# Last expert pair and output rows of a hybrid block: two quarters of the down product in a row, last rows scaled by VectorE

## The chip, the cores and the metric

The kernel is one launch on one core of a Trainium2 chip. The metric is the device time of a run in microseconds (us). PE is TensorE (matrix products into PSUM), DVE is VectorE, ACT is ScalarE, POOL is GpSimd, and SP is the engine that here only issues DMAs. Each engine takes its instructions in the order in which they were written, and waits on semaphores where an operand comes from another engine or from a DMA.

## The reference, cut to what matters

The input is 256 tokens of width 1024. Attention and a state-space mixer come first and are not touched. The end is a mixture of experts, then a gated projection and a norm:

```python
x = x + (gate_a * y_a + gate_b * y_b) @ w_out[i]
h2 = rms_norm(x, ffn_norm_g[i])
x = x + hier_moe(h2, ...)          # 16 experts: out += combine[e] * (silu(h @ w_gate[e]) * (h @ w_up[e])) @ w_down[e]
x = x + jax.nn.sigmoid(x @ w_ple_gate[i]) * (p[i] @ w_ple_proj[i])
return rms_norm(x, final_norm_g)
```

## The kernel before, in words

Tokens lie in two tiles of 128 (index `i`). The 16 experts are worked through in 8 pairs. For each pair the kernel gathers up to 64 tokens an expert, multiplies by gate and up (`gate_up`, L1078), transposes the hidden activations (`hidden_T`, L1097 and L1098), multiplies by down, splits the result into a rounded high part `yh` and a remainder `yl`, and scatters both back into four PSUM banks `x2_0` to `x2_3` (tile 0 and 1, left and right half of the columns) with a one-hot matrix. A pair's scatter (L1125) stands in the next pair's turn.

The last pair is done by quarters of 256 columns. `q_down(q)` is the down product of a quarter (L1429) with ACT making `yh` (L1434) and DVE making `yl` (L1435). `q_x2(q)` scatters it (L1441) and lets DVE add the residual `xt` (L1445). `q_T(q)` transposes the new residual (L1451) and splits it into `x2h` on ACT (L1453) and `x2l` on DVE (L1454). Then the gate product `x @ w_ple_gate` can use that quarter as rows of its contraction: its weights come in eight blocks `pg_0` to `pg_7` (block c has quarter c % 4 of the rows, and half c // 4 of the columns). `pg_split(c)` rounds a block on ACT (`wh_pg`, L329) and takes the remainder on DVE or, for blocks 4, 1 and 6, on POOL (`wl_pg`, L332). `pg(c, i, j)` issues the three products high by high, high by low, low by high (L341 to L343) for two rows of blocks.

`pg_gate` is the sigmoid (ACT, L1479), the product with `p @ w_ple_proj` and the sum with `xt` (DVE, L1480 and L1481). `pg_sq` squares and sums (ACT, L1490, for the last quarter DVE, L1488), `pg_sum` adds the parts (L1493), `pg_pow` raises to the power -1/2 on POOL (L1498), `pg_gain` multiplies by the norm's gain (L1501), and `finish` scales by the row's factor and stores: left half on ACT (L1505), right half on DVE (L1506), stores (L1509) by SP, and for the left half of tile 1 by ACT. The right half of tile 1 is done in two quarters (j = 0 and 1), the second one in a bank of its own, `pge`.

Behind all this stands a branch (L1155) that skips the work for experts with more than 64 tokens. PE, ACT, DVE and POOL each carry it, and SP then waits for all stores and all engines (L1599).

The order is the order of the calls in the code. Weights are streamed by SP alone, in the order of a list (`pending`), in which `LAST` says which gate blocks follow each quarter of down. A DMA is issued when a buffer of the ring of 51 is free and the eighth DMA before it has landed.

Of the kernel before, what the change touches and what calls it, by code (L numbers as in the profile page):

```python
# [11 lines left out]
AF = mybir.ActivationFunctionType  # L12
# [13 lines left out]
NPAIR = NE // 2  # L26
WARM = 10
PG_POOL = (4, 1, 6)
LAST = ((4,), (0,), (5, 1), (2, 6, 3, 7))
DFF = 512  # L30
IF_ENGINES = [mybir.EngineType.PE, mybir.EngineType.Activation, mybir.EngineType.DVE, mybir.EngineType.Pool]
IN_DIM = 6160
# [58 lines left out]
def emit(ctx, tc, ring, x, p, mix_norm_g, w_in, conv_w, conv_b, dt_bias,  # L91
# [1023 lines left out]
            dve.scalar_tensor_tensor(mo["yl"][:, sl], by[hf], cw, mo["yh"][:, sl].bitcast(F32), op0=OP.mult,  # L1115
                                     op1=OP.subtract)

    def scatter(pr, mo, st, tiles):
        for i in tiles:
            for hf in range(2):  # L1120
                for n, y in enumerate(("yh", "yl")):
                    j, first = 2 * i + hf, pr == 0 and n == 0
                    if first:
                        bx[j] = bank(j, f"x2_{j}")
                    pe.matmul(bx[j], st[:, i * P:(i + 1) * P], mo[y][:, 512 * hf:512 * hf + 512],  # L1125
                              start=first, stop=False, skip_group_check=True)
# [258 lines left out]
    for pr in range(NPAIR):  # L1385
        if pr == 2:
            MO["most"] = nc.values_load(cnt[0:1, 16:17], IF_ENGINES, min_val=0, max_val=T)
        if 0 < pr < NPAIR - 2 and pr % 2 == 0:
            for i in range(2):
                onehots(pr // 2 + 1, i)  # L1390
        st, cw = gate_up(pr, mo, first_pair() if pr == 0 else None)
        if pr % 2 == 1:
            XT[pr // 2].free()
        for i in range(2):

            if pr == 1:
# [12 lines left out]
        if pr == 0:  # L1409
            pp_end()  # L1410
        if pr < NPAIR - 1:
            down(pr, mo, cw)
        pend = (pr, st)
    table(AF.Sigmoid)
    MO["S"].free()
# [7 lines left out]
        return slice(256 * q, 256 * q + 256)  # L1423

    def q_down(q):
        b = bank(4, f"y7{q}")
        for c in range(4):
            for s in range(2):
                pe.matmul(b[64 * s:64 * s + 64, 0:256], mo["hT"][:, c, 64 * s:64 * s + 64],  # L1429
                          ready[f"d{NE - 2 + s}_{q}"][0][:, c, :], start=(c == 0), stop=(c == 3), skip_group_check=True)  # L1430
        for s in range(2):
            consumed(f"d{NE - 2 + s}_{q}")
        h, l = mo["yh"][:, quarter(q)], mo["yl"][:, quarter(q)]
        act.activation(h, b[:, 0:256], AF.Copy, scale=cw)  # L1434
        dve.scalar_tensor_tensor(l, b[:, 0:256], cw, h.bitcast(F32), op0=OP.mult, op1=OP.subtract)  # L1435
# [37 lines left out]
    def pg_cols(hf, j):  # L1473
        return slice(512 * hf, 512 * hf + 512) if j is None else quarter(2 * hf + j)

    def pg_gate(i, hf, j=None):
        sl = pg_cols(hf, j)
        t = sc.t[i][:, sl]
        act.activation(t, pgb[i, hf, j][:, sl.start - 512 * hf:sl.stop - 512 * hf], AF.Sigmoid)  # L1479
        dve.tensor_tensor(t, t, pp["t"][i][:, sl], OP.mult)  # L1480
        dve.tensor_tensor(t, t, xt[i][:, sl], OP.add)  # L1481

    def pg_sq(i, hf, j=None):

        sl, c = pg_cols(hf, j), 32 + 4 * i + hf + (j or 0)
        t, b, a = sc.t[i][:, sl], pgb[i, hf, j][:, sl.start - 512 * hf:sl.stop - 512 * hf], stat[:, c:c + 1]
        if j == 1:
            dve.scalar_tensor_tensor(b, t, 1.0 / D, t, op0=OP.mult, op1=OP.mult, accum_out=a)  # L1488
        else:
# [7 lines left out]
        r = stat[:, 40 + i:41 + i]  # L1497
        pool.tensor_tensor(r, r, nhalf[:, :1], OP.pow)  # L1498

    def pg_gain(i, sl):  # L1500
        dve.tensor_tensor(sc.t[i][:, sl], sc.t[i][:, sl], ready["fng"][0][:, 0, sl], OP.mult)  # L1501

    def finish(i):
        r = stat[:, 40 + i:41 + i]
        act.activation(sc.t[i][:, 0:512], sc.t[i][:, 0:512], AF.Copy, scale=r)  # L1505
        dve.tensor_scalar(sc.t[i][:, 512:1024], sc.t[i][:, 512:1024], r, None, op0=OP.mult)  # L1506
        for h in (1, 0):
            s = slice(512 * h, 512 * h + 512)
            (act if i > h else sp).dma_start(dram(out, i * P * D + 512 * h, [[D, P], [1, 512]]), sc.t[i][:, s])  # L1509

    q_down(0)
    pg_split(4)
    q_x2(0)
    q_T(0)
    pg_split(0)
    q_down(1)
    pg(4, 0)
    pg(4, 1, 0)
    q_x2(1)
    q_T(1)  # L1520
# [52 lines left out]
    for a in [X[0], X[1]] + [MO[n, i] for n in ("h2h", "h2l") for i in range(2)]:
# [29 lines left out]
```

## Time and profile before

| | us |
|---|---|
| median of 3 runs | 502.16 (501.2 to 502.59) |
| profiled execution | 501.87 |
| its span, first to last instruction | 500.1 |
| PE busy in the span | 482.4 |
| DVE, ACT, POOL busy | 208.2, 190.1, 129.7 |

The span is 1.8 us shorter than the profiled execution's time; the rest lies around it. The granted clock of PE was 1.0 from 12 us on until PE had done its last product. The last pair's work begins at about 450 us; everything ahead of it is the same in both kernels. Times below are us from the span's start.

### The profile page before, as it was taken

To read this page: it belongs to the slowest core of one execution; us is meant where nothing else is said; L and a number is where in the kernel's file an instruction comes from. 1 tells how busy PE (TensorE), PEld (TensorE's weight loads), DVE (VectorE), ACT (ScalarE), POOL (GpSimd) and SP (SyncE) were. 2 spreads that over 40 slices of the span, in tenths; PEclk is the share of its full clock that TensorE was granted. 3 is DMA by queue.
4 is the path that set the end of the run, shared out by engine and by line. 5 is a ranking of instruction groups with operands and counts; after the bars stand their busy time and mean duration, and the time that the engine had idled before them with its cause. 6 is when DMAs were issued, how large, how long until landed. Compare 5 with 4: busy or idle time off the path is not lost.

```text
span 500.1 us, 7983 instructions
## 1 busy us (share of the span) xinstructions
PE 482.4 (96%) x3093; PEld 340.5 (68%) x3093; DVE 208.2 (42%) x407; ACT 190.1 (38%) x344; POOL 129.7 (26%) x83
## 2 busy tenths in 40 slices
PE   6999999999999999999999999999999999999992
PEld 6997988999988999988744353434434353335682
DVE  4324678795669484744631111111201010103465
ACT  4747576644686273443531111110202020104442
POOL 3767546333887640060300000000000000001201
PEclk8999999999999999999999999999999999999997
DMA  8899999612323798677658999999999999999602
GB/s 288 233 318 348 348 348 283 209 43 87 102 88 124 256 393 289 207 252 293 251 209 312 368 410 408 409 410 408 409 408 409 408 409 409 409 389 364 222 0 90
DMA packets 71221, 145.25 MB, mean 290 GB/s; under 512 B 8244, under 2 KB 41352, under 8 KB 71176
## 3 DMA queue, kind: packets, MB, share of 16 engines
q1 hardware_dynamic: 70888, 143.89, 79.5%
q10 hardware_dynamic: 288, 0.79, 0.4%
q8 instruction: 26, 0.43, 0.3%
q14 instruction: 19, 0.16, 0.1%
HBM read 143.61 MB, written 1.05 MB: 289 GB/s over the span
## 4 chain that ended last, share of the span: by engine, by line
PE 88%; DVE 6%; ACT 2%; issue 2%; DMA 1%; POOL 0%; DVEq 0%; ACTq 0%; POOLq 0%
PE u L1078 11%; PE g L1078 11%; PE y L1108 10%; PE ac_gb L363 5%; PE ac_ob L363 5%; PE ac_ga L363 5%; PE g L1024 3%; PE ac_xs L363 3%; PE x L1125 3%; PE ac_bc L363 2%; PE ac_q L363 2%; PE ac_z L363 2%; PE ac_k L363 2%; PE y L1429 2%; PE pg L341 1%
## 5 line engine op out<-in xcount | busy, mean ns | idle before, releaser
L332 POOL TENSOR_TENSOR wl_pg<-pg,wh_pg 128x1024 fp32r<-128x1024 f32 x3 | 7.2, 2395 | 226.0 <-PE x L1441 213.7
L1078 PE MATMUL u<-u,XT 128*64 128x512 f32 x256 | 57.2, 595 | 0.0
L1078 PE MATMUL g<-g,XT 128*64 128x512 f32 x256 | 56.8, 593 | 0.0
L1108 PE MATMUL y<-d,mid 128*64 128x512 f32 x224 | 49.6, 595 | 0.0
L1078 PEld LDWEIGHTS g<-g,XT 128*64 128x64 f32 x256 | 18.1, 137 | 35.4 <-issue 32.9
L1078 PEld LDWEIGHTS u<-u,XT 128*64 128x64 f32 x256 | 17.9, 137 | 33.6 <-issue 30.2
L1115 DVE SCALAR_TENSOR_TENSOR yl<-y,cwt,yh 128x512 fp32r<-128x512 f32 x14 | 10.5, 750 | 60.2 <-ACT yh L1114 59.4
L1108 PEld LDWEIGHTS y<-d,mid 128*64 128x64 f32 x224 | 15.5, 137 | 29.4 <-issue 25.7
L1091 DVE SCALAR_TENSOR_TENSOR mid<-u,cwt,mid 128x512 f32<-128x512 f32 x8 | 6.0, 751 | 54.1 <-issue 47.4
L1098 ACT ACTIVATE mid<-hT 128x512 f32<-128x512 f32 x8 | 4.8, 598 | 55.0 <-PE hT L1097 55.0
L1114 ACT ACTIVATE yh<-y,cwt 128x512 fp32r<-128x512 f32 x14 | 9.6, 687 | 40.4 <-PE y L1108 40.4
L332 POOL TENSOR_TENSOR wl_xs<-xs,wh_xs 128x1024 fp32r<-128x1024 f32 x8 | 19.1, 2391 | 17.7 <-ACT wh_xs L329 8.0
L1053 ACT ACTIVATE sT<-st 128x256 fp32r<-128x256 f32 x8 | 3.1, 385 | 54.1 <-DVE cwt L1052 51.7
L1050 DVE COPY cwt<-st 128x1 f32<-128x1 f32 x8 | 1.3, 158 | 42.9 <-PE st L1045 42.9
L711 POOL TENSOR_TENSOR su<-su,su 128x768 f32<-128x768 f32 x8 | 16.9, 2108 | 7.6 <-ACT su L710 7.1
L1024 PE MATMUL g<-S,h2h 128*128 128x256 f32 x60 | 15.4, 291 | 0.6 <-ACT XT L1032 0.6
L332 POOL TENSOR_TENSOR wl_wo<-wo,wh_wo 128x1024 fp32r<-128x1024 f32 x3 | 7.8, 2613 | 31.0 <-ACT wh_wo L329 29.6
L1032 ACT ACTIVATE XT<-g,gfd 128x256 f32<-128x256 f32 x16 | 6.7, 470 | 23.4 <-PE g L1024 22.2
L1024 PE MATMUL g<-S,h2l 128*128 128x256 f32 x60 | 14.8, 281 | 0.0
L1024 PEld LDWEIGHTS g<-S,h2h 128*128 128x128 f32 x60 | 11.3, 188 | 4.1 <-issue 2.4
L332 POOL TENSOR_TENSOR wl_z<-z,wh_z 128x1024 fp32r<-128x1024 f32 x4 | 9.6, 2401 | 16.3 <-ACT wh_z L329 7.1
L341 PE MATMUL pg<-wh_pg,x2h 128*128 128x512 f32 (+1 forms) x32 | 12.3, 383 | 0.0
(392 smaller groups left out, 1178.7 us busy)
## 6 DMA issues: line engine op xcount, KB each, us to landing
g<-in_w_gate_dram SPq DMA_DIRECT2D x64, 512.0 KB, 10.2
u<-in_w_up_dram SPq DMA_DIRECT2D x64, 512.0 KB, 10.2
d<-in_w_down_dram SPq DMA_DIRECT2D x64, 512.0 KB, 10.2
xs<-in_w_in_dram SPq DMA_DIRECT2D x8, 512.0 KB, 8.8
z<-in_w_in_dram SPq DMA_DIRECT2D x8, 512.0 KB, 8.7
ga<-in_w_in_dram SPq DMA_DIRECT2D x8, 512.0 KB, 8.7
gb<-in_w_in_dram SPq DMA_DIRECT2D x8, 512.0 KB, 7.4
ob<-in_w_out_b_dram SPq DMA_DIRECT2D x8, 512.0 KB, 3.4
```

The lines of the kernel that those rows point to most:

```text
L332: (pool if pool_lo else dve).tensor_tensor(l, src, h.bitcast(F32), OP.subtract)
L341: pe.matmul(o, lh, rh, start=start, stop=False, skip_group_check=skip)
L363: pe.matmul(st["b"][:, T * f:T * f + T], w[:, k, 128 * f:128 * f + 128], x_.k(kk), start=(n + kk + f == 0), stop=(n == 2 and kk == 4 * k_u ...
L711: pool.tensor_tensor(e, e, cbm[:, t // 4:t // 4 + 1, :].to_broadcast([P, 2, 384]), OP.mult)
L1024: pe.matmul(b[:, 256 * k:256 * k + 256], MO[hs, i].t[0][:, kk * P:(kk + 1) * P], S, start=(first and n == 0 and k == 0), stop=(last and n ...
L1032: act.activation(o[:, 256 * k:256 * k + 256], b[:, 256 * k:256 * k + 256], AF.Copy, scale=g2[:, k:k + 1])
L1078: pe.matmul(b[64 * s:64 * s + 64, :], xg.k(kk)[:, s0 + 64 * s:s0 + 64 * s + 64], ws[s][:, k, :], start=(kk == 0), stop=(kk == KD - 1), ski ...
L1108: pe.matmul(by[hf][64 * s:64 * s + 64, :], mo["hT"][:, c, 64 * s:64 * s + 64], w[:, 0, 512 * hf:512 * hf + 512], start=(c == 0), stop=(c = ...
L1114: act.activation(mo["yh"][:, sl], by[hf], AF.Copy, scale=cw)
L1115: dve.scalar_tensor_tensor(mo["yl"][:, sl], by[hf], cw, mo["yh"][:, sl].bitcast(F32), op0=OP.mult, op1=OP.subtract)
L1125: pe.matmul(bx[j], st[:, i * P:(i + 1) * P], mo[y][:, 512 * hf:512 * hf + 512], start=first, stop=False, skip_group_check=True)
L1429: pe.matmul(b[64 * s:64 * s + 64, 0:256], mo["hT"][:, c, 64 * s:64 * s + 64], ready[f"d{NE - 2 + s}_{q}"][0][:, c, :], start=(c == 0), sto ...
```

## The change

1. The scatter of pair 6 is issued in another order: left halves of both tiles, the transposes of the hidden activations, the right half of tile 0, and the right half of tile 1 only after the scatter of quarter 0.
2. Quarter 1's down product follows quarter 0's at once, in a bank of its own. `LAST` loads its weights ahead of `pg_4`.
3. Gate products stand between the steps: `pg(4, 0)` ahead of the transposes of quarter 1, `pg(4, 1, 0)` behind them; the scatter of quarter 2 comes ahead of `pg(5, 1, 0)`, not behind.
4. The first quarter of the right half of tile 1 keeps its sum in PSUM (`pg_x3`) and its squares go to SBUF.
5. Tile 0 is scaled by factor and gain in one DVE instruction a half; tile 1 is scaled by DVE alone. ACT's two scales (L1505) are gone. SP issues all four stores.

```diff
-LAST = ((4,), (0,), (5, 1), (2, 6, 3, 7))
+LAST = ((), (4, 0), (5, 1), (2, 6, 3, 7))
...
+        if pr == NPAIR - 1:
+            scatter(pend[0], mo, pend[1], (0, 1), (0,))
+            hidden_T(pr, mo)
+            scatter(pend[0], mo, pend[1], (0,), (1,))
+            break
...
-        b = bank(4, f"y7{q}")
+        b = accbank("y71") if q == 1 else bank(4, f"y7{q}")
...
+    def pg_x3(i, hf, j):
+
+        sl = pg_cols(hf, j)
+        if j != 0:
+            return sc.t[i][:, sl]
+        return pgb[i, hf, j][:, sl.start - 512 * hf:sl.stop - 512 * hf]
+
...
-        dve.tensor_tensor(t, t, xt[i][:, sl], OP.add)
+        dve.tensor_tensor(pg_x3(i, hf, j), t, xt[i][:, sl], OP.add)
...
-    def finish(i):
-        r = stat[:, 40 + i:41 + i]
-        act.activation(sc.t[i][:, 0:512], sc.t[i][:, 0:512], AF.Copy, scale=r)
-        dve.tensor_scalar(sc.t[i][:, 512:1024], sc.t[i][:, 512:1024], r, None, op0=OP.mult)
-        for h in (1, 0):
-            s = slice(512 * h, 512 * h + 512)
-            (act if i > h else sp).dma_start(dram(out, i * P * D + 512 * h, [[D, P], [1, 512]]), sc.t[i][:, s])
+    def store(i, h):
+        s = slice(512 * h, 512 * h + 512)
+        sp.dma_start(dram(out, i * P * D + 512 * h, [[D, P], [1, 512]]), sc.t[i][:, s])
...
     q_down(0)
     pg_split(4)
+    q_down(1)
     q_x2(0)
+    scatter(pend[0], mo, pend[1], (1,), (1,))
     q_T(0)
+    q_x2(1)
     pg_split(0)
-    q_down(1)
     pg(4, 0)
-    pg(4, 1, 0)
-    q_x2(1)
     q_T(1)
     pg_split(5)
+    pg(4, 1, 0)
...
     pg(5, 0)
+    q_x2(2)
     pg(5, 1, 0)
-    q_x2(2)
...
-    finish(0)
+    for h in range(2):
+        s = slice(512 * h, 512 * h + 512)
+        dve.scalar_tensor_tensor(sc.t[0][:, s], sc.t[0][:, s], stat[:, 40:41], ready["fng"][0][:, 0, s], op0=OP.mult,
+                                 op1=OP.mult)
+        store(0, h)
...
+    pg_gain(1, 1, 0)
+    pg_gain(1, 1, 1)
+    for h in (1, 0):
+        s = slice(512 * h, 512 * h + 512)
+        dve.tensor_scalar(sc.t[1][:, s], sc.t[1][:, s], r, None, op0=OP.mult)
+        store(1, h)
```

PE, from the last products of `gate_up` on, in the kernel before (`x_0` to `x_3` are the scatter's banks, `hT` the transposed hidden activations, `y` a quarter of down, `x2T` the transposed residual; each `y` row has seven more like it):

```order
L1125 MATMUL x_1_3233<-yh_3103,sT_3044 128x512
...
L1097 MATMUL hT_4111<-ident,mid_3038 128x128 x4
L1125 MATMUL x_2_3263<-yh_3103,sT_3044 128x512
...
L1125 MATMUL x_3_3266<-yh_3103,sT_3044 128x512
...
L1429 MATMUL y_4122<-d_0_3960,mid_3038 64x256
...
L1441 MATMUL x_0_3230<-yh_3103,sT_3044 128x256
...
L1451 MATMUL x2T_4143<-ident,x_66 128x128 x2
...
L1429 MATMUL y_4156<-d_1_3970,mid_3038 64x256
```

The same place in the changed kernel:

```order
L1097 MATMUL hT_4111<-ident,mid_3038 128x128 x4
L1125 MATMUL x_1_3233<-yh_3103,sT_3044 128x512
...
L1433 MATMUL y_4120<-d_0_3960,mid_3038 64x256
...
L1433 MATMUL y_4135<-d_1_3968,mid_3038 64x256
...
L1445 MATMUL x_0_3230<-yh_3103,sT_3044 128x256
...
L1125 MATMUL x_3_3266<-yh_3103,sT_3044 128x512
...
L1455 MATMUL x2T_4154<-ident,x_66 128x128 x2
```

Both quarters of `y` now stand ahead of the first `x_0` of a quarter, and the products into `x_3` stand between that scatter and the transposes.

ACT at the same place, before:

```order
L1434 ACTIVATE yh_3103<-y_4122,cwt 128x256
L329 ACTIVATE wh_pg_4133<-pg_3968 128x1024
L1453 ACTIVATE x2h_4148<-x2T_4143 128x512
L329 ACTIVATE wh_pg_4152<-pg_3989 128x1024
L1434 ACTIVATE yh_3103<-y_4156,cwt 128x256
```

And in the changed kernel:

```order
L1438 ACTIVATE yh_3103<-y_4120,cwt 128x256
L329 ACTIVATE wh_pg_4131<-pg_3987 128x1024
L1438 ACTIVATE yh_3103<-y_4135,cwt 128x256
L1457 ACTIVATE x2h_4159<-x2T_4154 128x512
L329 ACTIVATE wh_pg_4169<-pg_3989 128x1024
```

The second `yh` now stands ahead of the first `x2h`, behind the rounding of block `pg_4`; on DVE the second `yl` likewise stands ahead of the two residual adds of quarter 0.

DVE at the end, from the last quarter's sum to the branch, before:

```order
L1488 SCALAR_TENSOR_TENSOR pge,stat<-sc_4350 128x256
L1567 TENSOR_TENSOR stat<-stat 128x1
L1501 TENSOR_TENSOR sc_4350<-sc_4350,fng 128x512
L1506 TENSOR_SCALAR sc_4350<-sc_4350,stat 128x512
L1155 COMPARE_AND_BRANCH
```

And in the changed kernel:

```order
L1501 SCALAR_TENSOR_TENSOR pge,stat<-sc_4350 128x256
L1580 TENSOR_TENSOR stat<-stat 128x1
L1515 TENSOR_TENSOR sc_4350<-pg_4191,fng 128x256
L1515 TENSOR_TENSOR sc_4350<-sc_4350,fng 128x256
L1586 TENSOR_SCALAR sc_4350<-sc_4350,stat 128x512 x2
L1155 COMPARE_AND_BRANCH
```

One gain of 512 columns became two of 256, the first of them with its operand in PSUM, and DVE has the left half's scale that ACT had.

## Rows read from the trace of the kernel before

**Rows 1.** Chain of waits: start us, us, engine, tile, line.

```profile
453.28 1.90 PE y L1429 x16
...
455.27 0.48 ACT yh L1434
...
457.98 1.88 PE y L1429 x16
...
460.29 0.23 PE pg L342
...
466.43 1.88 PE y L1429 x16
...
478.86 0.44 PE x2T L1451 x4
```

**Rows 2.** Timeline of PE, transposes of quarter 0; in brackets idle before.

```profile
457.21 0.77 PE L1451 MATMUL x2T<-ident,x 128*128 128x128 f32 x4 [0.28 <-DVE x L1445]
```

**Rows 3.** Groups by line, 443 to 501 us: count, then busy us, mean ns, idle before.

```profile
L329 ACT ACTIVATE wh_pg<-pg 128x1024 fp32r<-128x1024 f32 x8 | 8.3, 1050 | 0.0
...
L332 POOL TENSOR_TENSOR wl_pg<-pg,wh_pg 128x1024 fp32r<-128x1024 f32 x3 | 7.2, 2395 | 226.0 <-PE x L1441 213.7 <-ACT wh_pg L329 12.2
...
L1445 DVE TENSOR_TENSOR x<-x,x 128x256 f32<-128x256 f32 x8 | 3.0, 419 | 4.0 <-PE x L1441 4.0
...
L1454 DVE TENSOR_TENSOR x2l<-x2T,x2h 128x512 fp32r<-128x512 f32 x4 | 2.8, 692 | 3.2 <-ACT x2h L1453 3.1
...
L1453 ACT ACTIVATE x2h<-x2T 128x512 fp32r<-128x512 f32 x4 | 2.4, 598 | 9.5 <-PE x2T L1451 8.1 <-DMA d<-in_w_down_dram 1.3
...
L1435 DVE SCALAR_TENSOR_TENSOR yl<-y,cwt,yh 128x256 fp32r<-128x256 f32 x4 | 1.9, 482 | 9.0 <-ACT yh L1434 9.0
```

**Rows 4.** First two blocks of the last down weights: issue by SP, time to landing.

```profile
L155 SPq DMA_DIRECT2D d<-in_w_down_dram x2: 379/379/379, 439.9 to 441.2; - x2
...
DMA to landing us min/median/max: 10.4/10.5/10.6
```

**Rows 5.** Timeline of SP: the issue of block pg_4 in the third place.

```profile
442.44 3.15 SPq L155 DMA_DIRECT2D pg<-in_w_ple_gate_dram  x1
```

**Rows 6.** Timeline of DVE at the end.

```profile
488.47 1.35 DVE L1501 TENSOR_TENSOR sc<-sc,fng 128x256 f32<-128x256 f32 x3
...
491.65 0.41 DVE L1480 TENSOR_TENSOR sc<-sc,pp 128x256 f32<-128x256 f32 x1
...
493.16 0.69 DVE L1501 TENSOR_TENSOR sc<-sc,fng 128x512 f32<-128x512 f32 x1
494.28 0.49 DVE L1506 TENSOR_SCALAR sc<-sc,stat 128x512 f32<-128x512 f32 x1 [0.44 <-POOL stat L1498]
```

**Rows 7.** Timeline of POOL: the power of tile 1, and one at 242 us.

```profile
493.32 0.92 POOL L1498 TENSOR_TENSOR stat<-stat,nhalf 128x1 f32<-128x1 f32 x1 [4.04 <-DVE stat L1567]
...
242.47 0.55 POOL L917 TENSOR_TENSOR stat<-stat,nhalf 128x1 f32<-128x1 f32 x1
```

**Rows 8.** Timeline of ACT: the last quarter's sigmoid and ACT's store.

```profile
491.12 0.36 ACT L1479 ACTIVATE sc<-pge 128x256 f32<-128x256 f32 x1
...
495.03 0.36 ACTq L1509 DMA_DIRECT2D out_dram<-sc  x1
```

**Rows 9.** The branch at L1155 by engine: ns min/median/max, first and last start us.

```profile
L1155 DVEq EVENT_SEMAPHORE  x2: 21/21/21, 497.4 to 497.5; - x2
L1155 ACTq EVENT_SEMAPHORE  x2: 17/17/17, 498.8 to 498.9; - x2
...
L1155 DVEq COMPARE_BRANCH  x1: 72/72/72, 494.3 to 494.3; - x1
L1155 ACTq COMPARE_BRANCH  x1: 54/54/54, 495.4 to 495.4; - x1
```

**Rows 10.** SP's own waits at the end (total us, times, longest).

```profile
SPq L1599 <- ACTq L1155: 0.9, 1, 0.9
```

**Rows 11.** SP's stores: time from issue to landing, of one with a known landing.

```profile
DMA to landing us min/median/max: 2.3/2.3/2.3
```

More of the change, by code (lines that the diff above doesn't have):

```diff
@@ L1116, in down, with scatter @@
                                      op1=OP.subtract)
-    def scatter(pr, mo, st, tiles):
+    def scatter(pr, mo, st, tiles, halves=(0, 1)):
         for i in tiles:
-            for hf in range(2):
+            for hf in halves:
                 for n, y in enumerate(("yh", "yl")):
@@ L1410, in emit @@
             pp_end()
-        if pr < NPAIR - 1:
-            down(pr, mo, cw)
+        down(pr, mo, cw)
         pend = (pr, st)
@@ L1480, in pg_gate @@
         dve.tensor_tensor(t, t, pp["t"][i][:, sl], OP.mult)
-        dve.tensor_tensor(t, t, xt[i][:, sl], OP.add)
+        dve.tensor_tensor(pg_x3(i, hf, j), t, xt[i][:, sl], OP.add)
     def pg_sq(i, hf, j=None):
         sl, c = pg_cols(hf, j), 32 + 4 * i + hf + (j or 0)
-        t, b, a = sc.t[i][:, sl], pgb[i, hf, j][:, sl.start - 512 * hf:sl.stop - 512 * hf], stat[:, c:c + 1]
+        t, b, a = pg_x3(i, hf, j), pgb[i, hf, j][:, sl.start - 512 * hf:sl.stop - 512 * hf], stat[:, c:c + 1]
+        if j == 0:
+            b = sc.t[i][:, sl]
         if j == 1:
@@ L1498, in pg_pow, with pg_gain @@
         pool.tensor_tensor(r, r, nhalf[:, :1], OP.pow)
-    def pg_gain(i, sl):
-        dve.tensor_tensor(sc.t[i][:, sl], sc.t[i][:, sl], ready["fng"][0][:, 0, sl], OP.mult)
-    def finish(i):
-        r = stat[:, 40 + i:41 + i]
-        act.activation(sc.t[i][:, 0:512], sc.t[i][:, 0:512], AF.Copy, scale=r)
-        dve.tensor_scalar(sc.t[i][:, 512:1024], sc.t[i][:, 512:1024], r, None, op0=OP.mult)
-        for h in (1, 0):
-            s = slice(512 * h, 512 * h + 512)
-            (act if i > h else sp).dma_start(dram(out, i * P * D + 512 * h, [[D, P], [1, 512]]), sc.t[i][:, s])
+    def pg_gain(i, hf, j=None):
+        sl = pg_cols(hf, j)
+        dve.tensor_tensor(sc.t[i][:, sl], pg_x3(i, hf, j), ready["fng"][0][:, 0, sl], OP.mult)
+    def store(i, h):
+        s = slice(512 * h, 512 * h + 512)
+        sp.dma_start(dram(out, i * P * D + 512 * h, [[D, P], [1, 512]]), sc.t[i][:, s])
     q_down(0)
     pg_split(4)
+    q_down(1)
     q_x2(0)
+    scatter(pend[0], mo, pend[1], (1,), (1,))
     q_T(0)
+    q_x2(1)
     pg_split(0)
-    q_down(1)
     pg(4, 0)
-    pg(4, 1, 0)
-    q_x2(1)
     q_T(1)
     pg_split(5)
+    pg(4, 1, 0)
     pg_split(1)
@@ L1551, in emit @@
     pg_pow(0)
-    pg_gain(0, quarter(0))
-    pg_gain(0, quarter(1))
-    pg_gain(0, slice(512, 1024))
     for c in (6, 7):
@@ L1558, in emit @@
     pg_sq(1, 0)
-    finish(0)
+    for h in range(2):
[3 more added lines that the diff above has]
+        store(0, h)
     for c in (4, 5, 6, 7):
         pg(c, 1, 1)
-    pg_gain(1, slice(0, 512))
     pg_sq(1, 1, 0)
+    pg_gain(1, 0)
     pg_sum(1)
@@ L1566, in emit @@
     pg_sq(1, 1, 1)
-    dve.tensor_tensor(stat[:, 41:42], stat[:, 38:39], stat[:, 41:42], OP.add)
+    r = stat[:, 41:42]
+    dve.tensor_tensor(r, stat[:, 38:39], r, OP.add)
     pg_pow(1)
-    pg_gain(1, slice(512, 1024))
-    finish(1)
+    pg_gain(1, 1, 0)
[4 more added lines that the diff above has]
+        store(1, h)
     overflow()
```

## The prediction

> **What bounds the kernel now.** I read the chain of waits first, from the last pair on. It runs over PE almost without a break until the last gate product, then over ACT, DVE and POOL, one short instruction after the other, and then over the end of the program. So there are two places to look at: where PE stands still in the last pair, and what ends last behind it.
>
> PE stands still around each quarter. The down product of quarter 0 ends at 453.28 + 1.90 = 455.18; then ACT's high part and DVE's remainder must be made before quarter 0's scatter, and DVE's adds before the transposes [rows 1, 3]. The transposes of quarters 0, 1 and 2 each take 0.77 with 0.28 idle before them [rows 2], three such in all, while those of quarter 3, which have gate products between scatter and transposes, take 0.44 [rows 1]. The second `y` starts at 457.98, 2.8 after the first one ended, and the third at 466.43 [rows 1].
>
> At the end, DVE's and ACT's scales start at 494.28. ACT then issues a store at 495.03, branches at 495.4, and its next instruction starts at 498.8; DVE, which branches at 494.3, goes on at 497.4 [rows 6, 8, 9]. SP waited 0.9 for that step of ACT [rows 10], and the span ends 1.3 later, at 500.1. So the very end is ACT's last scale, its store and the stretch behind its branch.
>
> **Part 1, PE in the last pair.** PE's instructions are the same in number and shape, so only its waits change. I walk the new order with the old durations.
>
> The first `y` does not move: it waits for ACT's copy of the transposed activations, and those transposes still have four scatter products ahead of them. It ends at 455.18, its `yh` at 455.75, its `yl` at 456.24. The second `y` follows at once, 455.18 + 1.88 = 457.06, if its weights are there. The first two down blocks land at 439.9 + 10.4 = 450.3 and 441.2 + 10.6 = 451.8 [rows 4], so 1.5 apart; SP's queue is the same but for the order of three places, so I put the next two at 453.3 and 454.8 (an estimate from that spacing), just before they are wanted, and `pg_4` at 456.3.
>
> ACT now has the rounding of `pg_4` ahead of the second `yh`: 456.3 + 1.05 = 457.35 [rows 3], about 0.3 after the second `y` ends. `yh` ends at 457.83 (0.48), `yl` at 458.33 (0.48). DVE's two adds stand behind that `yl`: the first ends at 458.75, the second at 459.1 (0.42 each, overlapping by 0.07) [rows 1, 3]. PE has the scatter of quarter 0 and the two moved products into `x_3` meanwhile, some 4 x 0.12 + 2 x 0.23 = 0.94, and stands still from 458.0 to 458.8. Transposes to 459.57, `x2h` to 460.2 (0.60), under which quarter 1's scatter is hidden. Then `pg(4, 0)`: two products, a wait for `x2l` until 460.95 (0.69), four more at 0.23: 461.87. POOL's remainder of the block, 457.35 + 2.4 = 459.75, is there in time [rows 3]. Transposes of quarter 1 without a wait, 0.44: 462.3. `pg(4, 1, 0)`, six of half width, 0.7: 463.0. `pg(0, 0)` and `pg(0, 1)`, 12 x 0.23 = 2.76: 465.76. So the third `y` starts at about 465.8 where it started at 466.43: 0.65 gained.
>
> Quarter 2's transposes now have `pg(5, 1, 0)` between scatter and themselves, as quarter 3's have: at most 0.28 + 0.77 - 0.44 = 0.6 gained, at least the 0.28; I take 0.45. Behind that PE's order and its waits are the old ones. Sum for PE: **1.1**. The bounds are 0 (a `pg_4` one place later costs 1.5, which takes back both) and 1.6 (the walk overstates each hand-over by some tenths).
>
> **Part 2, the last rows on DVE and POOL.** All of this starts 1.1 earlier; I give it on the old clock. Before, tile 0's three gains took 1.35 from 488.47 on, and the last quarter's first product started at 491.65 [rows 6]. Now the gate of the quarter before it goes first, at 488.47, two instructions of 0.42 with a hand-over, to 489.3, when POOL's power is done too. Two instructions of three operands on 512 columns follow. The trace has none in SBUF alone: one on 256 columns took 0.48 and a plain product on 512 0.69 [rows 3, 6], so 0.69 is the floor and 0.96 the ceiling; I take 0.75, since going from 256 to 512 columns adds 0.27 (0.42 to 0.69). Less 0.08 of overlap each they end their turn at 490.65; the gain of tile 1's left half 0.61, the sum of its parts 0.12: the last quarter's product starts at 491.38, **0.27** earlier (0 to 0.4). ACT's sigmoid for it, 0.36, has no square ahead of it any more and ends before that [rows 8].
>
> Then the power of tile 1 on POOL. It took 0.92 beside DVE's gain of 512 columns, which ran from 493.16 to 493.85, and ended 0.40 after it; at 242 us, beside no such product, it took 0.55 [rows 6, 7]. Now the first gain of 256 columns reads PSUM, so the power should take 0.55. From the sum at 493.08 the scale started 1.20 later; now the two gains end 0.08 + 0.42 + 0.34 = 0.84 after it, the power 0.16 + 0.08 + 0.55 = 0.79, and the scale starts at 0.88: **0.32** earlier. If the second gain, which reads SBUF twice, is let in ahead of the power, the power ends 0.40 after it and the scale starts at 1.27: 0.07 lost. That is the other bound.
>
> Of these two bounds the Trainium skill has a rule (SBUF — State Buffer, "Who interferes with whom"): VectorE and GpSimd share a port pair, and whichever starts first keeps it for its whole instruction when VectorE has two SBUF inputs. The power's 0.92 agrees with that. By the rule taken to the letter the power would also hold up the second gain until it is done, and the scale would start some 0.23 later than I say. The trace speaks against that half: tile 0's three gains took 1.35 in all, no more than 0.42 + 0.42 + 0.69 with overlap, though tile 0's power ran beside them.
>
> **Part 3, the end.** DVE's two scales now run one after the other: from the first one's start 0.40 + 0.49 = 0.89 to the last end, where ACT's scale of the left half was there beside the right half's. SP issues the last store then; the one store with a known landing took 2.3 [rows 11], so it lands 3.2 after the start, 3.5 if a store takes a few tenths more. DVE's branch comes 0 to 0.4 after the first scale's start and its next instruction 3.1 after that [rows 9], so 3.1 to 3.5. Before, ACT's next instruction came at 498.8 - 494.28 = 4.5. ACT's new branch follows its last sigmoid, some 3 us before the scale, and is out of the way; its issue of a store, 0.36, is gone. Gained: 4.5 - 3.4 = **1.1** (1.0 to 1.4). What comes next is late by nothing else: SP's last waits and the final barrier, 1.3, stay.
>
> The four stores on one queue cost nothing that shows: two of them are tile 0's, issued some 3 us earlier, and the other two are 0.4 apart, about as long as one issue takes. Nothing else is queued behind them on SP.
>
> **Sum:** 1.1 + 0.27 + 0.32 + 1.1 = 2.8. The profiled execution took 501.87, so 499.1 by its own time; the median of the three runs is 0.3 above it, so I say **499.2**.
>
> **Rivals.**
>
> *The second quarter waits in ACT's queue.* The rounding of `pg_4` stands ahead of `yh` of quarter 1, and behind `yh` stand `yl`, both adds and the transposes. For it: in my walk the cast ends 0.3 after it should, with no slack at all. Against it: SP's places and landings are the old ones up to that block. One place later (1.5) PE gains nothing, 0.65 + 0.45 - 1.5 = -0.4, and the total gain is 1.3: 500.6.
>
> *The end does not shrink.* DVE's stretch behind its branch counts from the second scale's end, or the last store takes over a us longer than the one I can see. Then the 1.1 of part 3 is gone: 500.2.
>
> *The port by the letter.* The power holds up the second gain until its own end: the scale starts 0.23 later, 499.4. The skill's section named above is where this comes from.
>
> *Slower.* The same queue on ACT, but with a long hold on SP. The third place in SP's queue took 3.15 to issue before [rows 5], where others took 0.4. That hold is in my landings once; if `pg_4` meets one more such hold in the fifth place, and a place on top, it comes 3.15 + 1.5 = 4.65 later and everything behind it too: 501.87 - 2.8 + 4.65 = 503.7. It decides from a landing 2.8 later than 456.3, at 459.1; below that the change still gains.
>
> That the change does not do what it says is excluded by the order of instructions: the moved pieces are where the diff puts them on PE, ACT, DVE and SP.
>
> **How the numbers follow.** Forecast 0.56 (499.2), the port 0.15 (499.4), the wait on ACT 0.13 (500.6), the end 0.12 (500.2), slower 0.04 (503.7). A measurement of this kernel can tell about 0.3%, 1.5 us, from no change. The forecast and the port are faster by more than that; of the end's case, with 1.7 gained, I count two thirds so, and a fifth of the wait on ACT's, with 1.3: faster 0.82, same 0.14, slower 0.04. The range leaves out the slower case and a tail on each side: all terms at their best (1.6 + 0.4 + 0.32 + 1.4 = 3.7) give 498.2 to 498.5, and the wait on ACT gives 500.6: 498.2 to 500.7.
>
> **What would show it.** Right: the third `y` starts at 465.8 or a little earlier; quarter 2's transposes take 0.44 with no idle time; the power of tile 1 takes about 0.55; ACT's branch lies before POOL's power, and SP's last wait is for DVE or a store about 3.4 after the first scale's start. Wrong: a long wait of the second `yh` for the `pg_4` cast, with PE idle for over a us ahead of the first transposes; a power that still takes 0.9; or an end that is still 5.8 behind the scale's start.

## The result and the profile after

The changed kernel took 498.92 us (median; 498.04 to 499.49) beside 501.81 us of the kernel before: ratio 0.9944, 95% interval 0.9926 to 0.9962, clear of 1. A second time (e9_again) it was 499.47 beside 501.99, ratio 0.9938 (0.9913 to 0.9962). One of the six runs of the kernel before took 806.17 us: the median of 501.81 has it in (the other five have 501.46), the ratio leaves it out. The forecast was 499.2 us with a range of 498.2 to 500.7; the time lies in it, 0.3 below the forecast.

| | before | after |
|---|---|---|
| profiled execution, us | 501.87 | 498.22 |
| its span, us | 500.1 | 496.5 |
| from the first `y` of the last pair to the third `y` | 13.16 | 12.61 |
| ... to the fourth `y` | 20.25 | 19.09 |
| ... to the last sigmoid of 512 columns | 33.17 | 32.01 |
| ... to the first scale of tile 1 on DVE | 41.07 | 39.37 |
| ... to the span's end | 46.85 | 44.10 |

The two spans differ by 3.6, more than the medians do. The first `y` starts at 453.21 before and at 452.40 after, and in the further executions below anywhere between 451.72 and 454.20, whichever order follows it: what lies ahead of the last pair varies by that much. So every stretch from here on is measured from the start of the first `y`. From there the profiled executions differ by 46.85 - 44.10 = 2.75.

First PE in the last pair: the timeline of PE, before and then after (start, duration, engine, line, operation, count; in brackets the idle time ahead). The first row of before holds 16 products, that of after 32, since the second `y` follows at once.

```profile
453.21 1.95 PE L1429 MATMUL y<-d,mid 128*64 128x256 f32 x16
...
466.37 1.95 PE L1429 MATMUL y<-d,mid 128*64 128x256 f32 x16
471.37 0.77 PE L1451 MATMUL x2T<-ident,x 128*128 128x128 f32 x4 [0.28 <-DVE x L1445]
```

```profile
452.40 3.69 PE L1433 MATMUL y<-d,mid 128*64 128x256 f32 x32 [0.28 <-ACT mid L1098]
...
457.82 0.77 PE L1455 MATMUL x2T<-ident,x 128*128 128x128 f32 x4 [0.61 <-DVE x L1449]
...
465.01 1.95 PE L1433 MATMUL y<-d,mid 128*64 128x256 f32 x16
469.57 0.60 PE L1455 MATMUL x2T<-ident,x 128*128 128x128 f32 x4
471.49 1.95 PE L1433 MATMUL y<-d,mid 128*64 128x256 f32 x16
```

The idle 0.28 ahead of quarter 2's transposes is gone, and they overlap with the products around them, so that the chain of waits gives them 0.44. Ahead of quarter 0's transposes stands a new wait, 0.61, for DVE's adds. Behind it are ACT, DVE and POOL as follows, from the timelines after.

```profile
455.50 1.06 ACT L329 ACTIVATE wh_pg<-pg 128x1024 fp32r<-128x1024 f32 x1 [0.57 <-DMA pg<-in_w_ple_gate_dram]
456.46 0.46 ACT L1438 ACTIVATE yh<-y,cwt 128x256 fp32r<-128x256 f32 x1
...
456.95 0.48 DVE L1439 SCALAR_TENSOR_TENSOR yl<-y,cwt,yh 128x256 fp32r<-128x256 f32 x1 [1.51 <-ACT yh L1438]
457.35 0.74 DVE L1449 TENSOR_TENSOR x<-x,x 128x256 f32<-128x256 f32 x2
```

ACT waits for `pg_4`'s landing, rounds it, and only then makes the second `yh`; `yl` and the adds follow in a row on DVE.

Then the last rows on DVE and POOL, which answer [rows 6, 7]:

```profile
487.34 1.41 DVE L1569 SCALAR_TENSOR_TENSOR sc<-sc,stat,fng 128x512 f32<-128x512 f32 x2
...
489.40 0.42 DVE L1491 TENSOR_TENSOR sc<-sc,pp 128x256 f32<-128x256 f32 x1
...
490.83 0.16 DVE L1580 TENSOR_TENSOR stat<-stat 128x1 f32<-128x1 f32 x1
490.91 0.42 DVE L1515 TENSOR_TENSOR sc<-pg,fng 128x256 f32<-128x256 f32 x1
491.25 0.41 DVE L1515 TENSOR_TENSOR sc<-sc,fng 128x256 f32<-128x256 f32 x1
491.77 0.88 DVE L1586 TENSOR_SCALAR sc<-sc,stat 128x512 f32<-128x512 f32 x2
...
491.07 0.54 POOL L1511 TENSOR_TENSOR stat<-stat,nhalf 128x1 f32<-128x1 f32 x1 [3.77 <-DVE stat L1580]
```

And the end, which answers [rows 9, 10]: the branch by engine, and SP's own waits.

```profile
L1155 ACTq EVENT_SEMAPHORE  x2: 17/17/17, 491.4 to 491.4; - x2
L1155 DVEq EVENT_SEMAPHORE  x2: 21/21/21, 494.7 to 494.8; - x2
...
L1155 ACTq COMPARE_BRANCH  x1: 50/50/50, 488.7 to 488.7; - x1
...
L1155 DVEq COMPARE_BRANCH  x1: 72/72/72, 491.8 to 491.8; - x1
```

SP's last two stores, then its wait for the last of them:

```profile
492.28 0.81 SPq L1519 DMA_DIRECT2D out_dram<-sc  x2
```

```profile
SPq L1616 <- DMA out_dram<-sc: 0.4, 1, 0.4
```

ACT branches 3 us ahead of the scale and is back before it. SP no longer waits for ACT's or DVE's branch; its last wait ahead of the final barrier is for the last store, issued at 492.71 and seen landed at 495.34, 2.63 later.

### The profile page after: what moved, and what is told of

The parts are those of the page before. It is cut to its first block, busy times and chain, and to the rows that moved or that the text cites. A ratio compares the mean times of both kernels' runs of the same rounds, so it can differ in the third digit from the quotient of the medians.

```text
span 496.5 us, 7977 instructions
## 1 busy us (share of the span) xinstructions
PE 480.6 (97%) x3093; PEld 339.2 (68%) x3093; DVE 208.3 (42%) x407; ACT 188.7 (38%) x342; POOL 129.3 (26%) x83
## 3 DMA queue, kind: packets, MB, share of 16 engines
HBM read 143.61 MB, written 1.05 MB: 291 GB/s over the span
## 4 chain that ended last, share of the span: by engine, by line
PE 83%; DVE 6%; ACT 2%; DMA 2%; issue 1%; SPq 0%; POOL 0%; DVEq 0%; ACTq 0%
PE g L1078 11%; PE u L1078 11%; PE y L1108 10%; PE ac_gb L363 5%; PE ac_ob L363 5%; PE ac_ga L363 5%; PE g L1024 3%; PE ac_xs L363 3%; PE x L1125 2%; PE ac_bc L363 2%; PE ac_z L363 2%; DMA d<-in_w_down_dram 2%; PE pg L341 1%; PE pg L343 1%; PE pg L342 1%; PE wo L343 1%
```

## The experiments

Each edit is told against the kernel that its expectation names. Two runs of the changed kernel had medians 0.55 apart (498.92, 499.47), so terms of a few tenths can't be read from medians; they are read from the stretches of the trace. These repeat: in three executions with the old order of the pair the third `y` came 13.16, 13.17 and 13.18 behind the first, and in seven with the new order 12.43 to 12.66. That spread follows `pg_4`: in all seven the third `y` comes 9.51 to 9.53 behind the start of ACT's rounding of `pg_4`, and that starts 2.91 to 3.14 behind the first `y`, when the block has landed. All stretches are us from the first `y`; "sigmoid" is the last one of 512 columns, "scale" is DVE's first scale of tile 1.

| kernel | median | ratio to before (95%) | third y | fourth y | sigmoid | scale | end |
|---|---|---|---|---|---|---|---|
| before | 502.16 | | 13.16 | 20.25 | 33.17 | 41.07 | 46.85 |
| changed | 498.92 | 0.9944 (0.9926 to 0.9962) | 12.61 | 19.09 | 32.01 | 39.37 | 44.10 |
| e1_front | 500.21 | 0.9969 (0.9954 to 0.9984) | 12.49 | 18.98 | 31.89 | 39.80 | 45.59 |
| e2_tail | 499.94 | 0.9967 (0.9951 to 0.9983) | 13.17 | 20.26 | 33.20 | 40.55 | 45.42 |
| e3_end | 500.79 | 0.9970 (0.9956 to 0.9984) | 13.18 | 20.28 | 33.19 | 41.10 | 45.83 |
| e4_act_scale | 499.12 | 0.9941 (0.9921 to 0.9962) | 12.43 | 18.92 | 31.84 | 39.20 | 43.94 |
| e5_sbuf_gain | 498.52 | 0.9923 (0.9897 to 0.9950) | 12.52 | 19.01 | 31.92 | 39.28 | 44.26 |
| e6_no_t2 | 499.62 | 0.9952 (0.9929 to 0.9974) | 12.66 | 19.76 | 32.70 | 40.05 | 44.78 |
| e7_split_late | 498.87 | 0.9936 (0.9906 to 0.9967) | 12.97 | 19.45 | 32.36 | 39.72 | 44.41 |
| e8_adds_first | 497.71 | 0.9900 (0.9868 to 0.9931) | 11.98 | 18.46 | 31.38 | 38.73 | 43.41 |
| e9_again | 499.47 | 0.9938 (0.9913 to 0.9962) | 12.65 | 19.14 | 32.06 | 39.41 | 44.15 |
| e10_high_first | 498.29 | 0.9911 (0.9885 to 0.9936) | 11.66 | 18.15 | 31.07 | 38.43 | 43.42 |
| e11_act_store | 499.61 | 0.9944 (0.9923 to 0.9965) | 12.49 | 18.98 | 31.90 | 39.25 | 45.08 |
| e12_old_places | 499.49 | 0.9938 (0.9914 to 0.9963) | 13.16 | 19.65 | 32.56 | 39.92 | 44.70 |

### The two halves, and the end alone

e1_front puts the order of the last pair into the kernel before, with the bank and the places of `LAST`; e2_tail puts in the last rows and the stores. The first lines of e1_front's edit:

```diff
-LAST = ((4,), (0,), (5, 1), (2, 6, 3, 7))
+LAST = ((), (4, 0), (5, 1), (2, 6, 3, 7))
...
     q_down(0)
     pg_split(4)
+    q_down(1)
     q_x2(0)
+    scatter(pend[0], mo, pend[1], (1,), (1,))
     q_T(0)
+    q_x2(1)
...
```

> The kernel before with the new order of the last pair alone (down quarters, scatter, gate products, queue places); the last rows and the stores as before. Theory (part 1 of the sum is a term by itself): 1.1 us faster than the kernel before, up to 1.3, the third y about 0.65 earlier and quarter 2's transposes 0.44 long without idle time; the stretch from the last gate product to the span's end as before, 13.7 us. Rival (the last rows and the end hold all of the gain, PE's time in the pair is given back behind it): 0 to 0.3 us.

Measured: 500.21, that is 1.58 under the 501.79 of before, and by the stretches 46.85 - 45.59 = 1.26. It is all there at the sigmoid (33.17 - 31.89 = 1.28), and from the sigmoid to the end it is 13.7 in both. So PE's time in the pair is worth what it saves, and nothing behind it gives it back: the theory, with its upper value.

> The kernel before with the new last rows and stores alone; the last pair's down quarters in the old order. Theory: parts 2 and 3 of the sum, 0.27 + 0.32 + 1.1 = 1.7 us faster than the kernel before, and together with the other half of the change the whole 2.8 to 2.9. Rival (the terms are not additive, one of them only shows with the other): under 1.2 or over 2.3 us.

Measured: 499.94, 1.85 under before, and by the stretches 1.43, all of it behind the sigmoid: 0.52 ahead of the scale, where 0.59 was expected, and 0.91 behind it, where 1.1 was. The last store landed 2.77 after its issue here, 0.14 later than in the changed kernel. The halves add up: 1.26 + 1.43 = 2.69, against 2.75 of the whole change, as near as the landings of `pg_4` and of the last store let one read.

e3_end changes only who scales and stores tile 1:

```diff
-    finish(1)
+    for h in (1, 0):
+        s = slice(512 * h, 512 * h + 512)
+        dve.tensor_scalar(sc.t[1][:, s], sc.t[1][:, s], stat[:, 41:42], None, op0=OP.mult)
+        sp.dma_start(dram(out, P * D + 512 * h, [[D, P], [1, 512]]), sc.t[1][:, s])
```

> The kernel before, except that tile 1's two scales are both DVE's, one after the other, and both its stores SP's (tile 0's scale and stores as before). Theory (part 3): 1.1 us faster, ACT's branch ahead of POOL's power, from the first scale's start to the span's end 4.7 instead of 5.8. Rival (the end needs the scales ready early, and the second scale in a row costs what ACT's stretch gives back): 0 to 0.3 us faster.

Measured: 500.79, 1.00 under before; by the stretches 1.02, all behind the scale (45.83 - 41.10 = 4.73 instead of 5.78). The term of the end stands by itself.

### What in ACT's work at the end cost the time

> The changed kernel, except that the left half of tile 1 is scaled by ACT again, beside DVE's scale of the right half; SP still stores both. It parts ACT's scale from ACT's store in the term of the end. Theory (what counts is when ACT's last instruction before its branch starts): ACT's branch comes about 0.4 after the scale's start, its next instruction 2.6 to 3.4 behind that, so the end is about level with the last store's landing: 0 to 0.3 us slower than the changed kernel. Rival (ACT's store was what cost): 0.3 to 0.4 faster than the changed kernel, since the two scales run side by side. Second rival (any instruction of ACT this late costs the whole term): 1.1 slower.

```diff
-        dve.tensor_scalar(sc.t[1][:, s], sc.t[1][:, s], r, None, op0=OP.mult)
+        if h:
+            dve.tensor_scalar(sc.t[1][:, s], sc.t[1][:, s], r, None, op0=OP.mult)
+        else:
+            act.activation(sc.t[1][:, s], sc.t[1][:, s], AF.Copy, scale=r)
         store(1, h)
```

Measured: 499.12, from the scale to the end 4.74, as in the changed kernel (4.73). ACT's scale and the branch of e4_act_scale, by timeline and by line:

```profile
491.58 0.72 ACT L1589 ACTIVATE sc<-sc,stat 128x512 f32<-128x512 f32 x1 [2.55 <-POOL stat L1511]
...
L1155 ACTq EVENT_SEMAPHORE  x2: 17/17/17, 494.2 to 494.3; - x2
...
L1155 ACTq COMPARE_BRANCH  x1: 50/50/50, 491.6 to 491.6; - x1
```

ACT branches at the very start of its scale, not at its end, and is back at 494.2, ahead of DVE (494.7) and of the store. That the two scales run side by side gains nothing, since SP issues the two stores 0.42 apart in any case; so the 0.3 to 0.4 that the first rival promised did not come, though its cause, ACT's store, is borne out by the next run. The second rival, 1.1 slower, fell.

e11_act_store differs from this in one line, `act.dma_start` instead of SP's store for the left half:

> The changed kernel, except that the left half of tile 1 is scaled and stored by ACT, as in the kernel before. With ACT scaling and SP storing the end was as short as in the changed kernel. Theory (the store is the culprit: its issue waits for the scale's end, so ACT's branch comes 1.1 behind the scale's start, and its next instruction 2.6 to 3.4 behind that): from the scale's start to the span's end 5.1 to 5.8 instead of 4.7, 0.4 to 1.1 slower than the changed kernel, and SP's last wait is for ACT. Rival (the stores' landing sets the end in any case): 4.5 to 4.7, no difference or 0.2 faster, since the two stores go out side by side.

```profile
492.64 0.36 ACTq L1591 DMA_DIRECT2D out_dram<-sc  x1
...
L1155 ACTq EVENT_SEMAPHORE  x2: 17/17/17, 496.6 to 496.7; - x2
...
L1155 ACTq COMPARE_BRANCH  x1: 54/54/54, 493.0 to 493.0; - x1
```

```profile
SPq L1620 <- ACTq L1155: 1.1, 1, 1.1
```

Measured: from the scale to the end 45.08 - 39.25 = 5.83, as before the change (5.78); 0.98 slower by the stretches than the changed kernel, though its median, 499.61, is only 0.14 above that of e9_again beside it. The store waits in ACT's queue for the scale's end, the branch stands behind the store, and SP waits 1.1 for it. So ACT's store was the culprit; its scale was free.

The held branch is not all of it. ACT's next instruction comes 2.35 later than in e4_act_scale (496.57 and 494.22): 1.43 because the branch starts later, and 0.92 because the stretch behind it is longer (3.54 and 2.63). With a stretch of 2.63 ACT would have been back at about 495.65 (an estimate from these two runs), when SP saw the stores landed at 495.6; so nearly all of the lost 0.98 hangs on the longer stretch, whose cause no run shows.

### The power on POOL

e5_sbuf_gain lets `pg_x3` return the part of `sc` in SBUF for every quarter, so that both gains read SBUF twice; the squares of the first quarter go to PSUM again, as before the change. The part on `pg_x3`:

```diff
-        if j != 0:
-            return sc.t[i][:, sl]
-        return pgb[i, hf, j][:, sl.start - 512 * hf:sl.stop - 512 * hf]
+        return sc.t[i][:, sl]
```

> The changed kernel, except that the last two quarters' sums before the last gain stay in SBUF as in the kernel before, so both gains of 256 columns read SBUF twice. Theory (POOL's power is held up only by a VectorE product with two SBUF inputs): tile 1's power takes about 0.9 instead of 0.54, the first scale starts 1.2 instead of 0.94 behind the sum's start, and the rest is as in the changed kernel: 0.3 slower than it, 2.6 faster than the kernel before. Rival (the power was short because the product beside it is 256 columns long, or because another order lies around it): power 0.5 to 0.6 and no difference.

DVE's and POOL's timeline of e5_sbuf_gain:

```profile
491.05 0.16 DVE L1576 TENSOR_TENSOR stat<-stat 128x1 f32<-128x1 f32 x1
491.13 0.75 DVE L1511 TENSOR_TENSOR sc<-sc,fng 128x256 f32<-128x256 f32 x2
491.99 0.88 DVE L1582 TENSOR_SCALAR sc<-sc,stat 128x512 f32<-128x512 f32 x2
...
491.29 0.66 POOL L1507 TENSOR_TENSOR stat<-stat,nhalf 128x1 f32<-128x1 f32 x1 [3.77 <-DVE stat L1576]
```

Neither side is quite right. The power takes 0.66, more than 0.54 and less than 0.92. It ends 0.40 behind the first gain (491.13 + 0.42 = 491.55, then 491.95), the same 0.40 by which it outlasted the gain of 512 columns before the change [rows 6, 7]. But the scale starts 0.94 behind the sum, exactly as in the changed kernel (491.77 - 490.83): there DVE's second gain ends last (491.66, the power 491.61), here the power (491.95, the second gain 491.88), by less than the hand-over. The shorter gain is what counts; that it reads PSUM saves 0.12 on POOL and nothing at the scale. The end, 0.25 later behind the scale than in the changed kernel, is the last store's (landed 2.88 after its issue, not 2.63). The trace of the kernel before had this case already, in tile 0: its first gain of 256 columns ran from 488.47 to 488.88 [rows 6], and the power beside it ended 0.40 later.

```profile
488.63 0.65 POOL L1498 TENSOR_TENSOR stat<-stat,nhalf 128x1 f32<-128x1 f32 x1 [12.47 <-DVE stat L1493]
```

### Quarter 2's transposes

e6_no_t2 puts `pg(5, 1, 0)` ahead of quarter 2's scatter again.

```diff
-    q_x2(2)
     pg(5, 1, 0)
+    q_x2(2)
```

> The changed kernel, except that the half-width gate product of block 5 stands ahead of quarter 2's scatter again. It takes the transposes' part of part 1 alone away. Theory: quarter 2's transposes take 0.77 behind 0.28 idle again, the stretch from the third to the fourth y is 7.1 instead of 6.5, and the kernel is 0.6 slower than the changed one, 2.3 faster than the kernel before. Rival (PE's time there is given back at the next wait): the last sigmoid of 512 columns comes at the same time, no difference.

The timeline of PE in e6_no_t2:

```profile
470.11 0.77 PE L1455 MATMUL x2T<-ident,x 128*128 128x128 f32 x4 [0.28 <-DVE x L1449]
472.21 1.95 PE L1433 MATMUL y<-d,mid 128*64 128x256 f32 x16
```

From the third to the fourth `y` it is 7.10 again instead of 6.48, and all of that is left at the end (44.78 against 44.10 and 44.15). The piece is worth 0.62, as expected.

### The second quarter: ACT's queue and SP's places

e7_split_late swaps `pg_split(4)` and `q_down(1)`, so that ACT makes the second `yh` ahead of `pg_4`'s rounding.

> The changed kernel, except that the rounding of block pg_4 stands behind the second yh on ACT, not ahead of it. Rival to the forecast (the second quarter waits in ACT's queue): yh starts 0.4 earlier, straight behind its down product, and so do the first transposes and all of PE behind them: 0.4 faster than the changed kernel. Theory: the transposes do start some 0.4 earlier, but POOL's remainder of pg_4, 2.4 long, starts 0.9 later, and the first gate product that needs it waits: 0.2 to 0.4 slower than the changed kernel at the third y.

PE, ACT and POOL of e7_split_late, from the timelines:

```profile
457.65 0.77 PE L1455 MATMUL x2T<-ident,x 128*128 128x128 f32 x4 [0.32 <-DVE x L1449]
...
460.24 0.50 PE L342 MATMUL pg<-wl_pg,x2h 128*128 128x512 f32 x1 [0.63 <-POOL wl_pg L332]
...
456.28 0.47 ACT L1438 ACTIVATE yh<-y,cwt 128x256 fp32r<-128x256 f32 x1 [1.22 <-PE y L1433]
...
457.80 2.38 POOL L332 TENSOR_TENSOR wl_pg<-pg,wh_pg 128x1024 fp32r<-128x1024 f32 x1 [214.91 <-ACT wh_pg L329]
```

The second `yh` starts 3.75 behind the first `y` instead of 4.06, and the transposes 5.12 instead of 5.42. Then PE waits 0.63 for POOL, and the third `y` is 0.3 to 0.5 later than in the kernels with the new order. The wait in ACT's queue exists (0.3), but taking it away costs more: the theory, 0.2 to 0.4 slower.

e12_old_places takes the changed kernel with the old `LAST`, `pg_4` ahead of the second quarter's blocks.

> The changed kernel with the queue places of the kernel before: pg_4 in SP's queue ahead of the second quarter's two down blocks. Theory (the second y starts straight behind the first only because its blocks were moved a place ahead): the second block lands one place later, about 1.3 to 1.5, the second y starts about 1.3 later than 1.78 behind the first, the first transposes and the third y 0.7 to 0.9 later: 0.7 to 0.9 slower than the changed kernel. Rival (the landings have slack, or the earlier pg_4 with its earlier remainder gives it back): the third y within 0.2 of the changed kernel's.

Its first two `y` on PE's timeline:

```profile
451.72 2.37 PE L1433 MATMUL y<-d,mid 128*64 128x256 f32 x18 [0.28 <-ACT mid L1098]
454.34 1.94 PE L1433 MATMUL y<-d,mid 128*64 128x256 f32 x14 [0.25 <-DMA d<-in_w_down_dram]
```

The second `y` breaks off after two products and waits for the other block. The third `y` comes 13.16 behind the first, where the changed kernel has 12.61 and 12.65: 0.5 to 0.55 later, and so is the end. The theory holds, with less than the 0.7 to 0.9 expected, since `pg_4` is rounded by then and the second `yh` no longer waits for it: it starts 4.60 behind the first `y`, 0.54 later than the 4.06 of the changed kernel. (The median, 499.49, is that of the changed kernel beside it, 499.47; half a microsecond does not show in it.)

### The wait that the new order made

e8_adds_first keeps the order on PE, ACT and SP, and lets quarter 0's scatter and adds be issued between the second `yh` and `yl`:

```diff
         act.activation(h, b[:, 0:256], AF.Copy, scale=cw)
+        if mid is not None:
+            mid()
...
-    q_down(1)
-    q_x2(0)
+    q_down(1, lambda: q_x2(0))
```

> The changed kernel, except that quarter 0's scatter and DVE's two adds stand ahead of the second yl on DVE (PE's, ACT's and SP's order are the same). It takes away the one wait of PE that the new order has made, about 0.6 ahead of the first transposes. Theory: the adds start right behind the scatter, the transposes 0.3 to 0.45 earlier, and the third y as much: 0.3 to 0.45 faster than the changed kernel, 3.2 to 3.3 faster than the kernel before. Rival (the first gate product waits for x2h, x2l or POOL's remainder of pg_4 anyway): no difference at the third y.

DVE and PE of e8_adds_first, from the timelines:

```profile
457.32 0.76 DVE L1451 TENSOR_TENSOR x<-x,x 128x256 f32<-128x256 f32 x2 [1.14 <-PE x L1447]
457.99 0.47 DVE L1441 SCALAR_TENSOR_TENSOR yl<-y,cwt,yh 128x256 fp32r<-128x256 f32 x1
...
457.82 0.74 PE L1457 MATMUL x2T<-ident,x 128*128 128x128 f32 x4
```

The adds come 4.18 behind the first `y` instead of 4.95, the transposes 4.68 instead of 5.42 and without idle time. The third `y` comes 11.98 behind the first, 0.63 earlier than in the changed kernel and 0.45 earlier than in the best execution of its order; the end is 0.69 earlier. That is more than the 0.3 to 0.45 expected, and not luck of the landing: `pg_4`'s rounding starts 3.15 behind the first `y`, as late as in any of the seven. The third `y` now comes 8.83 behind that rounding, as it does in e7_split_late, and in both the first gate product starts its second part when POOL's remainder is done.

e10_high_first adds one thing: the first gate product takes its two high-by-high products first, ahead of those that need POOL's remainder and `x2l`.

```diff
+        if (c, i) == (4, 0):
+            for n in range(3):
+                for k in range(2):
+                    pe.matmul(pgb[i, hf, j][:, w], (X2L if n == 2 else X2H).k(2 * q + k)[:, s],
+                              (b if n == 1 else a)[:, k, w], start=first and n == 0 and k == 0, stop=False,
+                              skip_group_check=True)
+            return
```

> The order in which quarter 0's adds stand ahead of the second yl, and besides the first gate product of pg_4 takes its two high-by-high products first, then the two with POOL's remainder, then the two with x2l. Theory (the product waits 0.4 for POOL's remainder of pg_4): 0.2 to 0.3 faster than with the adds alone, the stretch from the first y to the third 11.7 to 11.8 instead of 11.98; 0.8 to 0.9 faster than the changed kernel, 3.6 than the kernel before. Rival (x2l comes no earlier, so the rest waits for it): no difference to the adds alone, 0.6 faster than the changed kernel.

> The changed kernel as it is, once more, as the measure for the three beside it on the same chip. From the first y of the last pair to the span's end 44.0 to 44.1 us, where the kernel before takes 46.85; 2.8 us faster than the kernel before.

The third `y` comes 11.66 behind the first, 0.32 better, and the scale 38.43, 0.30 better than e8_adds_first. Of that, 0.09 is an earlier `pg_4` (its rounding starts at 3.06, not 3.15); counted from the rounding the third `y` gains 0.23 (8.60 and 8.83), inside the 0.2 to 0.3 expected. The end does not show it in the profiled execution (43.42 against 43.41), because its last store landed 2.89 after its issue where that of e8_adds_first took 2.58. Beside e9_again on the same chip the median is 498.29 against 499.47. Both versions lie 0.7 below the changed kernel by the stretch to the end; the intervals of their ratios overlap that of the changed kernel, so by the times alone the step from 0.994 to 0.990 is not settled.

## Why the prediction was right, and where it was not

**PE, 1.1 forecast, 1.16 measured** at the sigmoid (33.17 - 32.01; 1.1 to 1.3 in the other executions of this order, e6_no_t2 aside). The third `y` was put 0.65 earlier and came 0.55 (0.50 to 0.73 over the seven executions of this order). The walk held in its parts: the rounding of `pg_4` was to start 3.1 behind the first `y` (456.3) and started 3.10; the second `yh` was to start 4.14 behind it and did at 4.06; the transposes were to start 5.6 behind it and did at 5.42, with 0.61 of idle time where 0.8 stood in the walk. Quarter 2's transposes were under-sized: 0.45 taken, 0.6 found (e6_no_t2), which is the upper value, all of the idle time and all of the difference to 0.44. So the sum for PE came out by two misses of opposite sign, 0.10 too much and 0.17 too little.

**The last rows, 0.27 and 0.32 forecast, 0.28 and 0.26 measured.** From the last sigmoid of 512 columns to the last quarter's product it was 5.27 and is 4.99. From the sum to the scale it was 1.20 and is 0.94. The three-operand instruction takes 0.75 on 512 columns (1.41 for two with overlap), the value taken. It need not have been bounded from other shapes: the profile of the kernel before has a three-operand instruction on 512 columns, with one operand in PSUM:

```profile
L1115 DVE SCALAR_TENSOR_TENSOR yl<-y,cwt,yh 128x512 fp32r<-128x512 f32 x14 | 10.5, 750 | 60.2 <-ACT yh L1114 59.4
```

That the power would take 0.55 because the first gain reads PSUM was right (0.54, and 0.66 without it), but the gain at the scale does not hang on it: e5_sbuf_gain has the same 0.94. The first gain is shorter, and that suffices. The bound of 1.27, in which the power waits for the second gain too, did not come in either kernel. The 0.06 by which the term was over-sized is the hand-over to the scale, 0.11 behind the second gain (491.66 to 491.77), for which the sum had 0.04.

**The end, 1.1 forecast, 1.05 measured** (5.78 to 4.73 from the scale on; 1.02 in e3_end alone). Both candidates named were close: DVE is back 2.9 after its branch, at 494.7, and the last store is seen 0.6 later, 3.57 after the scale's start (forecast 3.4, bounds 3.1 to 3.5). The landing time was the term too short: 2.63 behind an issue at 0.94, where the sum had 2.3 [rows 11] behind 0.89 and its upper bound 2.6. The tail behind it, which was to stay at 1.3, is 1.16, and that gives 0.1 back: of the 1.05, 0.95 lies ahead of SP's release (4.52 to 3.57) and 0.10 behind it. So this term too is nearly right by two misses that nearly cancel. The forecast counted ACT's scale, store and stretch as one; the runs part them: the scale is free, and the store holds the branch back and has the longer stretch behind it.

**The rivals.** *The second quarter waits in ACT's queue* is half true: `yh` waits 0.3, as the walk had it, and there is no slack, since the third `y` follows `pg_4`'s rounding one for one (9.51 to 9.53 behind it in all seven). But no place is lost, and e7_split_late shows that the wait is the cheaper of two. The price of a place in SP's queue, 1.5 in the forecast, is only 0.5 when the place is taken from the second quarter's block (e12_old_places). *The end does not shrink* fell.

*The port by the letter* fell in this kernel: the second gain, with two SBUF inputs, ran from 491.25 to 491.66 beside the power (491.07 to 491.61), in 0.41, as long as the first gain with its PSUM input (0.42). Its price in the forecast, 0.23, is a little low: by the sum's own terms the second gain would have ended at 0.79 + 0.34 = 1.13 instead of 0.84, which is 0.29. The Trainium skill (SBUF — State Buffer, "Who interferes with whom") says that VectorE with two SBUF inputs contends with a GpSimd instruction that reads SBUF, and that the shared port pair is an exclusive lock. The trace agrees where the product had started first (the power ended 0.40 behind it, beside 512 columns and beside 256), and not where the power had.

*Slower* did not come. The third place in SP's queue was held again (3.15 before, [rows 5]), with a block of down in it now, and the fifth place, where `pg_4` stands, was held too, as SP's timeline after shows:

```profile
441.74 2.85 SPq L155 DMA_DIRECT2D d<-in_w_down_dram  x1
...
445.96 2.43 SPq L155 DMA_DIRECT2D pg<-in_w_ple_gate_dram  x1
```

The block of down still landed in time for the second `y`, and `pg_4` came when the walk had it. So this rival's condition, a hold in the fifth place, was met in good part (2.43), but not its price: a hold at the issue did not move the landing by its own length.

What the forecast did not see is that the idle time it counted ahead of the first transposes could be had: nothing but the order of two steps on DVE made it.

## What to carry to other kernels

Ask of each instruction that an engine still has to issue what stands behind it in that engine's queue: a store that waited for its data kept a branch from being reached (e11_act_store), while an arithmetic instruction in the same place let the branch start along with it (e4_act_scale). When two steps are put in a row on one engine, walk the other engines' queues too, since the second step's remainder now stands ahead of the first step's adds. And compare kernels that differ by tenths from a fixed instruction of the trace onward, not by spans or medians.

## What was not expected of the hardware

- An engine's branch starts while the instruction ahead of it still runs (ACT's branch at 491.6, its scale 491.58 to 492.30, in e4_act_scale); DVE's in the changed kernel (491.82) even comes ahead of its second scale (492.17). But a branch did not start before a DMA issue ahead of it had ended (493.02 after a store issued at 492.64 in 0.36, in e11_act_store).
- The time from ACT's branch to its next semaphore step was 2.56 to 3.11 in the eleven kernels in which no store of ACT's stood ahead (2.63 in the changed one), and 3.38, 3.40 and 3.54 in the three in which one did (before, e1_front, e11_act_store). The traces' DMA packets of the kind "instruction", of 8 KB each, fit this: in the eleven, one starts 0.92 to 1.49 after ACT's branch; in the three, none does, and the next one starts 1.8 after it, 0.04 to 0.3 before the store's own last packet has ended. That these packets are what ACT waits for, and that the store's data hold them up, is read from their times alone; no run tests it.
- The last store's landing, 2.58 to 2.89 after its issue in executions of the same end, is by now the largest single piece behind the scale, and its spread hides gains of 0.3.
